# Recurrent block: three output blocks taken from raw tokens and scaled in PSUM, the tokens normalised in place meanwhile

## The chip, the cores and the metric

The kernel runs on one core of one Trainium2 chip. The metric is the device time of one execution in microseconds, as the median of the runs. The engines are named as in the profile: PE (matmuls; PEld its weight loads), DVE (VectorE), ACT (ScalarE), POOL (GpSimd) and SP (which issues the DMAs; SPq is its queue).

## The reference

A two-layer trunk on 1024 tokens of width 1024, in float32. Layer one is a recurrent block and an MLP, layer two banded attention and an MLP; each part is normalised first and added to the stream. Only the recurrent block's beginning is touched:

```
def rmsnorm(x, g):
    y = xf * lax.rsqrt(jnp.mean(xf * xf, axis=-1, keepdims=True) + EPS)
    return (y * g.astype(jnp.float32)).astype(x.dtype)

def recurrent_block(x, w_in, conv_w, conv_b, w_gate, b_gate, lam, w_out):
    u = x @ w_in
    gate, rec = u[..., :D_RNN], u[..., D_RNN:]
    rec = causal_depthwise_conv(rec, conv_w, conv_b)
    h = rg_lru(rec, w_gate, b_gate, lam)
    return (jax.nn.gelu(gate) * h) @ w_out

h = h + recurrent_block(rmsnorm(h, a_norm[l]), a_w_in[l], ...)
```

The norm's factor, one number per token, is the same for all 1024 features of that token, so it can be multiplied into x before the product with w_in or into the product after it.

## The kernel before, in words

Everything lies transposed: features on the 128 partitions, tokens along the free axis. x is eight feature blocks (k = 0 to 7) of 1024 tokens, and each is handled as two halves (h = 0, 1) of 512 tokens. w_in has sixteen output blocks of 128 columns: eight for the gate, eight for the recurrence. The weights of one output block come in two halves of 128x512 (y = 0 for k = 0 to 3, y = 1 for k = 4 to 7).

Float32 products are made of three float32r matmuls: each operand is split into a high part (ACT, a copy that rounds, L487 for weights, L589 for tokens) and a low part (DVE, the difference, L489 and L592), and `mm` (L334 to L336) adds high by high, low by high and high by low in PSUM. One `mm` of 512 tokens is three matmuls; one output block over all k and both halves is 48.

The stage is written as many small chains (Python generators) that a planner, `Plan`, runs in the order of planned times. It gives every operation a cost and a due time (`a_`, `d_`, `p_` are the planned costs on ACT, DVE and POOL), flags and counting semaphores hold chains back, and the order in which the planner reaches the operations is the order in each engine's queue on the chip. The engines work their queues in order; the planner knows nothing of engines that hold one another up. Because the order is fixed at build time, an instruction that is late on the chip also holds what stands behind it in its queue.

The chains around the change:

- `loads` (L494) issues the DMAs on SP: first the first half of x (eight blocks), then the weights of the first two output blocks with the small vectors between them, then the second half of x with the third block's weights, then all other weights. Raw weights have three buffers (`NRAW_A`), and each is free again when DVE has made the low part.
- `square` (L538): ACT squares each token block, DVE adds the squares up (L551).
- `rstd` (L555): PE sums the squares over the partitions (L559), ACT takes Ln, Exp and a Square (L563, L565, L569), and DVE makes one Newton step (L571, L574), which gives R[h], the negated factor. It sets `normal[h]`.
- `halve` (L580): once the norm of half h is there, DVE multiplies the token block by R[h] in place (L585), ACT makes the high part times the negated gain (L589), DVE the low part (L592).
- `constants` (L414): some 25 instructions on 128x8 tiles, mostly on DVE (L416), among them a polynomial for softplus; the tanh and exponential of the recurrence use them (sp4, sp8).
- `tensor` (L712) is PE's order: the first three output blocks (recurrence 0 and 1, gate 0) go together through half 0 and then half 1, each in a PSUM tile of its own (`recs`); then a loop in which one recurrence block (n + 1) goes ahead, followed by the gate matmuls of recurrence n - 1 (L746) and a gate block. The fourth output block, the first in the loop, takes the same parts of the tokens as the first three. `block` (L691) goes through one output block by weight halves.
- `conv` (L596) takes a finished recurrence block out of PSUM with one ACT pass (L602) and three DVE passes (L609), and makes parts of the result (L618, L620); `gate` (L668) takes the gelu; `lru` (L624) makes the recurrence, on ACT, DVE and POOL.
- Before the first real work, PE runs 24 warm-up matmuls (`WARM`, L1293) on constants.

There are four PSUM tiles of 1024 columns in this stage, seven SBUF buffers for wide intermediate results (`bs`) and ten for split weights (`wss`).

Of the kernel before, what the change touches and what calls it, by code (L numbers as in the profile page):

```python
# [18 lines left out]
NF = 8  # L19
# [11 lines left out]
NW_A = 10  # L31
BANKS = {"pj": 2, "tp": 3, "po": 1, "sc": 2}
PIN = 0
WARM = 24
START = 48
SLACK = 14
ROWS = 2
# [120 lines left out]
def tile_yoco_rglru_chunk_attention(  # L158
# [42 lines left out]
    def gf(s="g"):  # L201
        return gp.tile([P, H2], F32, tag="g", name=nm(s))
# [34 lines left out]
    def hs(h):  # L237
        return slice(h * H2, (h + 1) * H2)
# [175 lines left out]
    def constants():  # L414
        def small(f, *args, **kw):
            f(*args, **kw)  # L416
            return plan.use("dve", 0.2)

        yield plan.t
        yield small(dve.tensor_scalar, gneg, vec[:, V_AN, :], -1.0, None, ALU.mult)  # L420
        dve.tensor_scalar(e0, lam, -1.0, None, ALU.mult)
# [3 lines left out]
        yield small(dve.tensor_scalar, e2, e1, 2.0, None, ALU.add)  # L425
        yield small(dve.reciprocal, e2, e2)
        yield small(dve.tensor_tensor, e1, e1, e2, ALU.mult)
        yield small(dve.tensor_tensor, e2, e1, e1, ALU.mult)
        yield small(dve.tensor_scalar, sps, e2, 1.0 / 19, 1.0 / 17, ALU.mult, ALU.add)
# [5 lines left out]
        yield small(dve.tensor_scalar, sp4, sps, 4.0, None, ALU.mult)  # L435
        yield small(dve.tensor_scalar, sp8, sps, -8.0, None, ALU.mult)
        yield arrived[NF - 1, 1]
        yield small(dve.tensor_scalar, gq, hn[:, 0:1], 0.125, None, ALU.mult)
        yield small(dve.tensor_scalar, gk, hn[:, 1:2], -1.0, None, ALU.mult)
# [17 lines left out]
    normal, gated = flags(2), flags(NF + 1)  # L457
    conved, posted, hidden, out_y = flags(NF), flags(NF + 2), flags(NF), flags(NF)
    xin, xsq, W, recs, C, HID, GW = {}, {}, {}, {}, {}, {}, {}
    Y = [[None, None] for _ in range(NF)]  # L460
# [31 lines left out]
        weighed[i, y].set(last)  # L492

    def loads():  # L494
        for k in range(NF):
            xin[k, 0] = gf("x")
            dma(xin[k, 0], xT[k, :, hs(0)])
            arrived[k, 0].set(plan.load(H2))
        for i in range(2):
            for y in range(2):  # L500
                yield raws
                load_half(i, y)
            if i == 0:
                dma(vec, vecs)
                plan.start(constants(), plan.load(NVEC * NF * 2) + 1.0)
        for k in range(NF):
            xin[k, 1] = gf("x")
            dma(xin[k, 1], xT[k, :, hs(1)])
            arrived[k, 1].set(plan.load(H2))
            if k == 3:  # L510
                dma(hn, hnorm)
                for y in range(2):
                    yield raws
                    load_half(2, y)
# [22 lines left out]

    def square(k, h):  # L538
        yield arrived[k, h]
        if (k, h) == (0, 1):  # L540
            yield normal[0,]
        elif h:
            yield squared[k - 1, h]
        yield bs
        q = bf("acc")[:, hs(0)]
        if k == 0:
            xsq[0, h] = q
        act.activation(q, xin[k, h], AF.Square)
        yield plan.use("act", a_(H2))
        if k:  # L550
            dve.tensor_tensor(xsq[0, h], xsq[0, h], q, ALU.add)  # L551
            bs.release(plan.use("dve", d_(H2)))
        squared[k, h].set(plan.busy["dve"] + LAT if k else plan.t)

    def rstd(h):  # L555
        yield squared[NF - 1, h]
# [20 lines left out]
        bs.release(last)  # L577
        normal[h,].set(last)

    def halve(k, h):  # L580
        yield normal[h,]
        if k:
            yield halved[k - 1, h]
        x = xin[k, h]
        dve.tensor_tensor(x, x, R[h], ALU.mult)  # L585
        yield plan.use("dve", d_(H2))
        hi, lo = gr("h"), gr("l")
        g = gneg[:, k : k + 1]
        act.activation(hi, x, AF.Copy, scale=g)  # L589
        X[k][h] = (hi, lo)  # L590
        yield plan.use("act", a_(H2))
        dve.scalar_tensor_tensor(lo, x, g, hi.bitcast(F32), ALU.mult, ALU.subtract)  # L592
        halved[k, h].set(plan.use("dve", d_(H2)))


    def conv(n, ps):  # L596
# [91 lines left out]
        xs.release(last)  # L688
        out_y[n,].set(last)

    def block(ps, i, Z, ks, start, stop):  # L691

        for y in range(2):
            mine = [k for k in ks if k // 4 == y]
            if not mine:
                continue
            yield weighed[i, y]
            for h in range(2):
                for k in mine:
                    if Z is Y:  # L700
                        yield out_y[k,]
                    w = W[i, y]
                    mm(
                        ps[:, hs(h)], (w[0][:, k % 4, :], w[1][:, k % 4, :]), Z[k][h],
                        start and k == ks[0], stop and k == ks[-1],
                    )
                    yield plan.pe(3 * H2) - LAT
            if i not in IN_G and mine[-1] % 4 == 3:
                wss.release(plan.now)
                wss.release(plan.now)  # L710

    def tensor():  # L712
# [575 lines left out]
    with tc.manual_schedule(engines=set(ENG)):  # L1288

        idle = bank2()[:, hs(0)]  # L1290
        wide = onesr.unsqueeze(1).broadcast_to([P, 4, P])
        for x in range(WARM):
            pe.matmul(idle, lhsT=onesr, rhs=wide, start=x == 0, stop=x == WARM - 1)  # L1293
        plan.start(loads())
        plan.start(gate_weights())
        for h in range(2):
            for k in range(NF):
                plan.start(square(k, h))
            plan.start(rstd(h))
            for k in range(NF):  # L1300
                plan.start(halve(k, h))
        plan.start(tensor())
        plan.start(o1.loads())
        plan.run()
# [497 lines left out]
```

## Time and profile before

| what | value |
|---|---|
| median of 3 runs (lowest, highest) | 2134.49 us (2132.64, 2136.97) |
| span of the profiled execution | 2134.0 us, 0.5 us under the median |
| PE, DVE, ACT, POOL busy in the span | 2091.0, 1546.1, 1106.3, 578.6 us |
| first 63 us: PE, DVE, ACT, POOL busy | 48.34, 43.56, 33.90, 2.81 us |
| first real matmul starts | 19.72 us |
| first gate matmul starts | 73.85 us |

A time is given from the start of the span. In a row of the timeline stand the start, the time that it took, the engine, the line of the kernel, the operation and its output and input tiles; in brackets the idle time of the engine before it and what ended that. In the table by stages, each engine's busy time stands with its count of instructions, then the granted PE clock (1.00 is full speed), the DMA share and the bandwidth. In the groups of instructions, the count is followed by the total, the mean in ns, and the idle time ahead. A row can carry the line of a helper: all three matmuls of a product have L334 to L336, whichever block they belong to.

### The profile page before, as it was taken

To read this page: it belongs to the slowest core of one execution; us is meant where nothing else is said; L and a number is where in the kernel's file an instruction comes from. 1 tells how busy PE (TensorE), PEld (TensorE's weight loads), DVE (VectorE), ACT (ScalarE), POOL (GpSimd) and SP (SyncE) were. 2 spreads that over 40 slices of the span, in tenths; PEclk is the share of its full clock that TensorE was granted. 3 is DMA by queue.
4 is the path that set the end of the run, shared out by engine and by line. 5 is a ranking of instruction groups with operands and counts; after the bars stand their busy time and mean duration, and the time that the engine had idled before them with its cause. 6 is when DMAs were issued, how large, how long until landed. Compare 5 with 4: busy or idle time off the path is not lost.

```text
span 2134.0 us, 29347 instructions
## 1 busy us (share of the span) xinstructions
PE 2091.0 (98%) x9768; PEld 1733.2 (81%) x9768; DVE 1546.1 (72%) x2602; ACT 1106.3 (52%) x1965; POOL 578.6 (27%) x511
## 2 busy tenths in 40 slices
PE   7999999999999999999999999989999999999999
PEld 5788787888888888887888888878778888888887
DVE  7777768777777776647777877767787777777743
ACT  5777635434434545546666666764544343444631
POOL 0123202333310000127666666650133332000000
PEclk9999999999999999999999999999999999999999
DMA  4111324544469784534323332343364445987732
GB/s 139 35 50 50 128 94 168 183 149 154 157 230 317 234 264 131 163 109 111 87 73 97 91 96 79 88 151 127 103 215 144 158 154 174 332 263 245 241 107 94
DMA packets 174296, 319.21 MB, mean 150 GB/s; under 512 B 20544, under 2 KB 22592, under 8 KB 174144
## 3 DMA queue, kind: packets, MB, share of 16 engines
q1 hardware_dynamic: 174144, 317.33, 45.8%
q8 instruction: 77, 1.26, 0.3%
q14 instruction: 75, 0.61, 0.1%
HBM read 219.73 MB, written 78.64 MB: 140 GB/s over the span
## 4 chain that ended last, share of the span: by engine, by line
PE 87%; DVE 6%; ACT 3%; issue 2%; DMA 1%; POOL 1%; SPq 0%; DVEq 0%; ACTq 0%; POOLq 0%
PE pj L334 12%; PE pj L336 11%; PE pj L335 11%; PE tp L334 6%; PE tp L336 6%; PE tp L335 6%; PE sc L336 4%; PE sc L335 4%; PE sc L334 4%; PE p L335 3%; PE p L334 3%; PE p L336 3%; PE tp L1583 2%; PE po L1611 2%; PE po L1610 1%
## 5 line engine op out<-in xcount | busy, mean ns | idle before, releaser
L334 PE MATMUL pj<-h,wh 128*128 128x512 f32 x1198 | 482.6, 403 | 4.5 <-DVE s L1118 3.7
L335 PE MATMUL pj<-l,wh 128*128 128x512 f32 x1198 | 468.7, 391 | 0.7 <-POOL l L1636 0.7
L336 PE MATMUL pj<-h,wl 128*128 128x512 f32 x1198 | 468.5, 391 | 0.2
L1037 ACT ACTIVATE wh<-raw 128x512 fp32r<-128x512 f32 x349 | 219.0, 629 | 318.2 <-PE po L335 80.6
L1038 DVE TENSOR_TENSOR wl<-raw,wh 128x512 fp32r<-128x512 f32 x349 | 270.2, 777 | 102.6 <-ACT wh L1037 99.1
L334 PEld LDWEIGHTS pj<-h,wh 128*128 128x128 f32 x1198 | 226.4, 189 | 48.3 <-DVE s L1118 4.9
L336 PEld LDWEIGHTS pj<-h,wl 128*128 128x128 f32 x1198 | 225.3, 188 | 49.0 <-DVE wl L1038 1.0
L335 PEld LDWEIGHTS pj<-l,wh 128*128 128x128 f32 x1198 | 226.6, 189 | 38.9 <-POOL l L1636 1.4
L334 PE MATMUL tp<-h,wh 128*128 128x512 f32 x569 | 221.8, 390 | 0.0
L335 PE MATMUL tp<-l,wh 128*128 128x512 f32 x569 | 221.6, 390 | 0.0
L336 PE MATMUL tp<-h,wl 128*128 128x512 f32 x569 | 221.6, 389 | 0.0
L348 DVE TENSOR_TENSOR l<-raw,h 128x512 fp32r<-128x512 f32 x224 | 154.1, 696 | 28.4 <-ACT h L347 26.9
L336 PE MATMUL sc<-h,wl 128*128 128x512 f32 x425 | 166.4, 392 | 0.0
L347 ACT ACTIVATE h<-raw 128x512 fp32r<-128x512 f32 x224 | 137.4, 620 | 56.1 <-DMA raw<-hid 32.7
L335 PE MATMUL sc<-l,wh 128*128 128x512 f32 x425 | 166.4, 391 | 0.0
L334 PE MATMUL sc<-h,wh 128*128 128x512 f32 x425 | 166.1, 391 | 0.0
L334 PE MATMUL p<-h,wh 128*128 128x512 f32 x384 | 151.7, 395 | 12.5 <-ACT h L589 8.1
L1119 ACT ACTIVATE s<-s 128x512 f32<-128x512 f32 x125 | 78.4, 629 | 164.4 <-DVE s L1118 164.4
L1046 POOL TENSOR_TENSOR raw<-raw,raw 128x512 f32<-128x512 f32 x30 | 49.7, 1657 | 405.3 <-DVE wl L1038 398.2
L335 PE MATMUL p<-l,wh 128*128 128x512 f32 x384 | 151.3, 394 | 3.0 <-DVE l L592 2.7
L336 PE MATMUL p<-h,wl 128*128 128x512 f32 x384 | 150.3, 391 | 0.0
L294 POOL TENSOR_TENSOR raw<-raw,vec 128x512 f32<-128x512 f32 x48 | 54.8, 1142 | 262.9 <-DVE l L348 259.6
(276 smaller groups left out, 4206.3 us busy)
## 6 DMA issues: line engine op xcount, KB each, us to landing
raw<-hid SPq DMA_DIRECT2D x224, 256.0 KB, 3.6
hid<-s SPq DMA_DIRECT2D x221, 256.0 KB, 2.1
raw<-in_w_down SPq DMA_DIRECT2D x192, 256.0 KB, 3.5
raw<-in_w_up SPq DMA_DIRECT2D x128, 256.0 KB, 2.6
s<-in_w_down SPq DMA_DIRECT2D x64, 256.0 KB, 4.3
raw<-in_w_in SPq DMA_DIRECT2D x32, 256.0 KB, 2.7
raw<-in_w_kv SPq DMA_DIRECT2D x32, 256.0 KB, 3.3
od<-ev SPq DMA_DIRECT2D x48, 128.0 KB, 2.2
```

The lines of the kernel that those rows point to most:

```text
L294: pool.tensor_tensor(raw, raw, gains, ALU.mult)
L334: pe.matmul(ps, lhsT=wh, rhs=xh, start=start, stop=False, skip_group_check=more)
L335: pe.matmul(ps, lhsT=wh, rhs=xl, start=False, stop=False, skip_group_check=more)
L336: pe.matmul(ps, lhsT=wl, rhs=xh, start=False, stop=stop, skip_group_check=more)
L347: act.activation(h, src, AF.Copy)
L348: dve.tensor_tensor(l, src, h.bitcast(F32), ALU.subtract)
L1037: act.activation(wh, raw, AF.Copy)
L1038: dve.tensor_tensor(wl, raw, wh.bitcast(F32), ALU.subtract)
L1046: pool.tensor_tensor(raw[A11], raw[A11], raw[A21], ALU.add)
L1119: act.activation(out, out, AF.Square)
L1583: pe.transpose(pt[:, g * P : (g + 1) * P], sc[:, (kb - kb0) * P : (kb - kb0 + 1) * P], ident)
L1611: pe.matmul(out, lhsT=st, rhs=pl[:, off : off + wid], start=False, stop=y == final)
```

## The change

The norm no longer stands ahead of the first three output blocks.

- `part` (new): as soon as a token block and the gains are there, ACT and DVE make the high and low parts of the raw tokens times the negated gain. The first three output blocks use these.
- `scaled_later` (new): when the three blocks are done, DVE multiplies each half of each of the three PSUM tiles by R[h], six instructions, and then the convolution or the gelu goes on as before.
- `halve`: the product with R[h] in place now waits also for `spent`, PE's use of the raw parts. It runs on POOL, but for k = 3 and 7 of the first half on DVE. ACT and DVE then make the parts again, in the same tiles. The fourth output block and all later ones use these.
- `square`: of the first half ACT still squares, and POOL adds; of the second half POOL squares and DVE adds.
- `constants`: most of the small instructions go from DVE to POOL.
- `loads`: the vectors go first, then tokens of the first half in turn with the weights of the first three blocks, then all of the second half.
- `block`: the fourth output block goes through half 0 and then half 1 over all k, and each product waits for its own parts.
- `WARM`: 12 rather than 24.

The diff, cut to its core:

```
-WARM = 24
+WARM = 12
...
+        def aside(f, *args, **kw):
+            f(*args, **kw)
+            return plan.use("pool", 0.25)
...
-        yield small(dve.tensor_scalar, gneg, vec[:, V_AN, :], -1.0, None, ALU.mult)
+        gained[0,].set(small(dve.tensor_scalar, gneg, vec[:, V_AN, :], -1.0, None, ALU.mult))
+        yield arrived[NF - 1, 0]
...
         for m in (15, 13, 11, 9, 7, 5, 3, 1):
-            yield small(dve.tensor_tensor, sps, sps, e2, ALU.mult)
-            yield small(dve.tensor_scalar, sps, sps, 1.0 / m, None, ALU.add)
+            yield aside(pool.tensor_tensor, sps, sps, e2, ALU.mult)
+            yield aside(pool.tensor_scalar, sps, sps, 1.0, 1.0 / m, ALU.mult, ALU.add)
...
     def loads():
...
+        dma(vec, vecs)
+        plan.start(constants(), plan.load(NVEC * NF * 2))
+        token_block(0, 0)
+        for y, ks in ((0, (1, 2, 3)), (1, (4, 5, 6))):
+            for i, k in zip(range(3), ks):
                 yield raws
                 load_half(i, y)
+                token_block(k, 0)
+        token_block(NF - 1, 0)
         for k in range(NF):
+            token_block(k, 1)
+        dma(hn, hnorm)
...
     def square(k, h):
...
-        act.activation(q, xin[k, h], AF.Square)
-        yield plan.use("act", a_(H2))
+        if h:
+            pool.tensor_tensor(q, xin[k, h], xin[k, h], ALU.mult)
+            yield plan.use("pool", p_(H2))
+        else:
+            act.activation(q, xin[k, h], AF.Square)
+            yield plan.use("act", a_(H2))
         if k:
-            dve.tensor_tensor(xsq[0, h], xsq[0, h], q, ALU.add)
+            (dve if h else pool).tensor_tensor(xsq[0, h], xsq[0, h], q, ALU.add)
...
+    def part(k, h):
+        yield gained[0,]
+        yield arrived[k, h]
         x = xin[k, h]
         hi, lo = gr("h"), gr("l")
         g = gneg[:, k : k + 1]
         act.activation(hi, x, AF.Copy, scale=g)
         X[k][h] = (hi, lo)
         yield plan.use("act", a_(H2))
         dve.scalar_tensor_tensor(lo, x, g, hi.bitcast(F32), ALU.mult, ALU.subtract)
+        parted[k, h].set(plan.use("dve", d_(H2)))
+
+    def halve(k, h):
+        yield normal[h,]
+        yield spent[k, h]
+        x = xin[k, h]
+        if not h and k % 4 == 3:
+            dve.tensor_tensor(x, x, R[h], ALU.mult)
+            yield plan.use("dve", d_(H2))
+        else:
+            pool.tensor_tensor(x, x, R[h], ALU.mult)
+            yield plan.use("pool", p_(H2))
+        hi, lo = X[k][h]
+        g = gneg[:, k : k + 1]
+        act.activation(hi, x, AF.Copy, scale=g)
+        yield plan.use("act", a_(H2))
+        dve.scalar_tensor_tensor(lo, x, g, hi.bitcast(F32), ALU.mult, ALU.subtract)
         halved[k, h].set(plan.use("dve", d_(H2)))
+
+    def scaled_later(ps, then):
+        for h in range(2):
+            yield normal[h,]
+            dve.tensor_tensor(ps[:, hs(h)], ps[:, hs(h)], R[h], ALU.mult)
+            yield plan.use("dve", d_(H2))
+        yield from then
...
     def tensor():
...
                 for x in range(3):
                     yield weighed[x, k // 4]
-                    yield halved[k, h]
+                    yield parted[k, h]
...
+                spent[k, h].set(plan.now)
...
-        plan.start(conv(0, recs[0]))
-        plan.start(gate(0, recs[2]))
-        plan.start(conv(1, recs[1]))
+        plan.start(scaled_later(recs[0], conv(0, recs[0])))
+        plan.start(scaled_later(recs[2], gate(0, recs[2])))
+        plan.start(scaled_later(recs[1], conv(1, recs[1])))
...
-                yield from block(ps, widx[NF + n + 1], X, allk, True, True)
+                yield from block(ps, widx[NF + n + 1], X, allk, True, True, n == 1)
```

More of the change, by code (lines that the diff above doesn't have):

```diff
@@ L417, in small @@
             return plan.use("dve", 0.2)
+        def aside(f, *args, **kw):
+            f(*args, **kw)
+            return plan.use("pool", 0.25)
         yield plan.t
[L420 to L421 removed]
+        gained[0,].set(small(dve.tensor_scalar, gneg, vec[:, V_AN, :], -1.0, None, ALU.mult))
+        yield arrived[NF - 1, 0]
+        yield aside(pool.tensor_scalar, e0, lam, -1.0, 1.0, ALU.mult, ALU.mult)
         yield small(dve.tensor_tensor, e1, e0, lam, ALU.max)
@@ L424, in constants @@
         yield plan.use("act", 0.25)
-        yield small(dve.tensor_scalar, e2, e1, 2.0, None, ALU.add)
+        yield aside(pool.tensor_scalar, e2, e1, 1.0, 2.0, ALU.mult, ALU.add)
         yield small(dve.reciprocal, e2, e2)
-        yield small(dve.tensor_tensor, e1, e1, e2, ALU.mult)
-        yield small(dve.tensor_tensor, e2, e1, e1, ALU.mult)
-        yield small(dve.tensor_scalar, sps, e2, 1.0 / 19, 1.0 / 17, ALU.mult, ALU.add)
+        yield aside(pool.tensor_tensor, e1, e1, e2, ALU.mult)
+        yield aside(pool.tensor_tensor, e2, e1, e1, ALU.mult)
+        yield aside(pool.tensor_scalar, sps, e2, 1.0 / 19, 1.0 / 17, ALU.mult, ALU.add)
         for m in (15, 13, 11, 9, 7, 5, 3, 1):
-            yield small(dve.tensor_tensor, sps, sps, e2, ALU.mult)
-            yield small(dve.tensor_scalar, sps, sps, 1.0 / m, None, ALU.add)
+            yield aside(pool.tensor_tensor, sps, sps, e2, ALU.mult)
+            yield aside(pool.tensor_scalar, sps, sps, 1.0, 1.0 / m, ALU.mult, ALU.add)
         yield small(dve.scalar_tensor_tensor, sps, sps, 2.0, e1, ALU.mult, ALU.mult)
         yield small(dve.scalar_tensor_tensor, sps, e0, 0.0, sps, ALU.max, ALU.add)
-        yield small(dve.tensor_scalar, sp4, sps, 4.0, None, ALU.mult)
-        yield small(dve.tensor_scalar, sp8, sps, -8.0, None, ALU.mult)
+        yield aside(pool.tensor_scalar, sp4, sps, 4.0, 1.0, ALU.mult, ALU.mult)
+        yield aside(pool.tensor_scalar, sp8, sps, -8.0, 1.0, ALU.mult, ALU.mult)
         yield arrived[NF - 1, 1]
-        yield small(dve.tensor_scalar, gq, hn[:, 0:1], 0.125, None, ALU.mult)
-        yield small(dve.tensor_scalar, gk, hn[:, 1:2], -1.0, None, ALU.mult)
+        yield aside(pool.tensor_scalar, gq, hn[:, 0:1], 0.125, 1.0, ALU.mult, ALU.mult)
+        yield aside(pool.tensor_scalar, gk, hn[:, 1:2], -1.0, 1.0, ALU.mult, ALU.mult)
     def a_(n):
@@ L456, in tile_yoco_rglru_chunk_attention @@
     weighed = flags(3 * NF, 2)
-    normal, gated = flags(2), flags(NF + 1)
+    normal, gained = flags(2), flags(1)
+    parted, spent = flags(NF, 2), flags(NF, 2)
     conved, posted, hidden, out_y = flags(NF), flags(NF + 2), flags(NF), flags(NF)
@@ L494, in loads, with token_block @@
     def loads():
[L495 to L500, printed above, removed]
+        def token_block(k, h):
+            xin[k, h] = gf("x")
+            dma(xin[k, h], xT[k, :, hs(h)])
+            arrived[k, h].set(plan.load(H2))
+        dma(vec, vecs)
[3 more added lines that the diff above has]
+            for i, k in zip(range(3), ks):
                 yield raws
                 load_half(i, y)
-            if i == 0:
-                dma(vec, vecs)
-                plan.start(constants(), plan.load(NVEC * NF * 2) + 1.0)
+                token_block(k, 0)
+        token_block(NF - 1, 0)
         for k in range(NF):
[L507 to L514, printed above, removed]
+            token_block(k, 1)
+        dma(hn, hnorm)
         for i in range(3, 3 * NF):
@@ L539, in square @@
         yield arrived[k, h]
[L540 to L543, printed above, removed]
         yield bs
@@ L547, in square @@
             xsq[0, h] = q
-        act.activation(q, xin[k, h], AF.Square)
-        yield plan.use("act", a_(H2))
+        if h:
[4 more added lines that the diff above has]
+            yield plan.use("act", a_(H2))
         if k:
-            dve.tensor_tensor(xsq[0, h], xsq[0, h], q, ALU.add)
-            bs.release(plan.use("dve", d_(H2)))
-        squared[k, h].set(plan.busy["dve"] + LAT if k else plan.t)
+            (dve if h else pool).tensor_tensor(xsq[0, h], xsq[0, h], q, ALU.add)
+            last = plan.use("dve", d_(H2)) if h else plan.use("pool", p_(H2))
+            bs.release(last)
+        squared[k, h].set(last if k else plan.t)
     def rstd(h):
@@ L578, in rstd @@
         normal[h,].set(last)
[L580 to L583, printed above, removed]
+    def part(k, h):
+        yield gained[0,]
+        yield arrived[k, h]
         x = xin[k, h]
-        dve.tensor_tensor(x, x, R[h], ALU.mult)
-        yield plan.use("dve", d_(H2))
         hi, lo = gr("h"), gr("l")
@@ L689, in gate, with block @@
         out_y[n,].set(last)
[L691 to L696, printed above, removed]
-            yield weighed[i, y]
[L698 to L708, printed above, removed]
+    def block(ps, i, Z, ks, start, stop, halves=False):
+        ys = [[k for k in ks if k // 4 == y] for y in range(2)]
+        if halves:
+            order = [(h, k) for h in range(2) for k in ks]
+        else:
+            order = [(h, k) for mine in ys for h in range(2) for k in mine]
+        for h, k in order:
+            y = k // 4
+            yield weighed[i, y]
+            if Z is Y:
+                yield out_y[k,]
+            else:
+                yield halved[k, h]
+            w = W[i, y]
+            mm(
+                ps[:, hs(h)], (w[0][:, k % 4, :], w[1][:, k % 4, :]), Z[k][h],
+                start and k == ks[0], stop and k == ks[-1],
+            )
+            yield plan.pe(3 * H2) - LAT
+            if i not in IN_G and h == 1 and k == ys[y][-1] and k % 4 == 3:
                 wss.release(plan.now)
@@ L1300, in tile_yoco_rglru_chunk_attention @@
             for k in range(NF):
+                plan.start(part(k, h))
+            for k in range(NF):
                 plan.start(halve(k, h))
```

## The prediction

> **What bounds the kernel now.** I read the page first, then the busy time by stages, then the waits, then the single instructions of the first 100 us.
>
> ```profile
> span 2134.0 us, 29347 instructions
> PE 2091.0 (98%) x9768; PEld 1733.2 (81%) x9768; DVE 1546.1 (72%) x2602; ACT 1106.3 (52%) x1965; POOL 578.6 (27%) x511
> core 0: us, PE busy (x) PEld busy (x) DVE busy (x) ACT busy (x) POOL busy (x), PEclk, DMA share, GB/s
> 0.00:5.00 5.00, 4.02 (x10) 3.15 (x11) 0.00 (x0) 2.41 (x3) 1.24 (x11) 1.00 0.51 166
> 10.00:15.00 5.00, 1.12 (x2) 0.30 (x2) 4.17 (x9) 4.02 (x9) 0.00 (x0) 0.87 0.46 148
> 15.00:20.00 5.00, 0.28 (x1) 0.28 (x1) 4.20 (x12) 3.04 (x5) 0.00 (x0) 0.50 0.78 219
> 20.00:25.00 5.00, 4.18 (x9) 2.49 (x9) 3.11 (x7) 2.33 (x4) 0.00 (x0) 0.60 1.04 369
> 45.00:63.00 18.00, 18.00 (x81) 14.86 (x81) 11.03 (x17) 7.82 (x11) 0.00 (x0) 1.00 0.08 28
> 90.30:93.60 3.30, 0.07 (x2) 0.07 (x1) 3.30 (x4) 3.06 (x4) 2.20 (x3) 1.00 0.29 89
> 93.60:200.00 106.40, 106.40 (x470) 88.12 (x470) 81.39 (x70) 79.52 (x88) 25.92 (x13) 1.00 0.16 51
> ```
>
> PE is the bound, at 98% of the span. All that the change can touch lies before about 94 us: from 93.6 to 200 PE is busy 106.40 of 106.40 us. So whatever moves PE's arrival there moves the end by as much. The last row also gives the pace of a matmul: 106.40 / 470 = 0.226 us.
>
> Two rows date PE's work in the recurrent block, and two its waits:
>
> ```profile
> 19.72 0.79 PE L334 MATMUL p<-h,wh 128*128 128x512 f32 x1 [6.30 <-ACT h L589]
> 73.85 0.39 PE L334 MATMUL p<-ch,gw 128*128 128x512 f32 x1
> PE p L334 <- ACT h L589: 8.1, 4, 6.3
> PE p L334 <- DVE c L609: 3.2, 1, 3.2
> ```
>
> The first real matmul starts at 19.72, after the norm of the first half. The first gate matmul starts at 73.85. Ahead of it stands the fourth output block (48 matmuls, 10.9 us, so it began at 63.0), and ahead of that the first three (144 matmuls, 32.6 us, from 19.72 to 63.0: 10.7 us of it waits and the slow clock of the rows from 15 to 25). 73.85 is my yardstick: the time at which the changed kernel reaches the same gate matmul.
>
> **The change part by part.** *PE's start.* The first three blocks no longer wait for the norm. They wait for the gains, one half block of tokens and a split weight.
>
> ```profile
> 3.88 1.23 ACT L548 ACTIVATE acc<-x 128x512 f32<-128x512 f32 x2 [1.87 <-DMA x<-in_xT]
> 6.91 3.93 ACT L548 ACTIVATE acc<-x 128x512 f32<-128x512 f32 x6 [1.80 <-DMA x<-in_xT]
> vec<-in_vecs SPq DMA_DIRECT2D x1, 52.0 KB, 4.7
> L589 ACT ACTIVATE h<-x,gneg 128x512 fp32r<-128x512 f32 x16 | 11.4, 720 | 17.6 <-DVE x L585 17.6
> ```
>
> The vectors now go first: issued at 0.7, landing 4.7 later, 5.4; gains and high part (0.72) after it: about 6.3; the first tokens are there before that (ACT squares them from 3.88). Twelve warm-up matmuls at the pace of the first ten (4.02 / 10 = 0.4 us in the row from 0 to 5, from about 1.0 on) end at about 5.8, so halving the warm-up costs nothing. With 32.6 us of work PE could be through with three blocks at about 40 to 45, some 18 to 20 us earlier. That is the gain on offer. But the fourth block takes normalised tokens, as all later ones do, and needs the last low part of the second half's eighth block. So the yardstick is set by how fast DVE, ACT and POOL make two complete sets of parts in place of one.
>
> *What DVE and POOL have to do.* Before, DVE did the products with the norm, the additions of squares, the low parts and the weights' low parts. Now POOL does 7 additions, 8 squares and 14 of 16 products, and DVE 16 more low parts. The question is whether the two run side by side. The trace has stretches in which both are loaded:
>
> ```profile
> 359.44 1.61 POOL L1049 TENSOR_TENSOR raw<-raw,raw 128x512 f32<-128x512 f32 x1 [3.10 <-DVE wl L1038]
> 359.82 1.78 DVE L1038 TENSOR_TENSOR wl<-raw,wh 128x512 fp32r<-128x512 f32 x1
> 361.13 1.62 POOL L1051 TENSOR_TENSOR raw<-raw,raw 128x512 f32<-128x512 f32 x1
> 361.52 1.78 DVE L1168 TENSOR_TENSOR raw<-raw,raw 128x512 f32<-128x512 f32 x1
> 371.25 1.59 POOL L1047 TENSOR_TENSOR raw<-raw,raw 128x512 f32<-128x512 f32 x1
> 371.63 0.68 DVE L1154 TENSOR_TENSOR s<-pj,s 128x512 f32<-128x512 f32 x1
> 41.76 1.29 DVE L585 TENSOR_TENSOR x<-x,rneg 128x512 f32<-128x512 f32 x2
> 43.24 1.42 DVE L592 SCALAR_TENSOR_TENSOR l<-x,gneg,h 128x512 fp32r<-128x512 f32 x2 [0.19 <-ACT h L589]
> L1058 POOL TENSOR_TENSOR raw<-raw,raw 128x512 f32<-128x512 f32 x1 | 1.3, 1302 | 4.4 <-DMA raw<-in_w_up 4.4
> L1389 POOL TENSOR_TENSOR s<-q x32: 1034/1042/1487, 951.2 to 1376.3; 128x512 f32<-128x512 f32 x32
> ```
>
> Around 360 the two take turns: each DVE instruction with both inputs in SBUF grows from 0.69 to 1.78 us and ends 0.55 after POOL's, and each POOL instruction from 1.30 to 1.61. One of each costs 361.13 - 359.44 = 1.69 us. At 371.63 a DVE instruction whose one input is PSUM runs through a POOL instruction at its usual 0.68. So DVE instructions with two SBUF inputs and POOL's exclude one another. Alone, DVE's follow at 1.29 - 0.69 = 0.60 us and the low parts at 1.42 - 0.75 = 0.67, which leaves 1.69 - 0.60 = 1.09 for POOL's. A square (one tensor read twice) takes 1.04 rather than 1.30; less the same 0.2 of overhead, 0.84.
>
> The Trainium skill states the same ("SBUF — State Buffer", section "Who interferes with whom"): a VectorE instruction with two SBUF inputs and a GpSimd instruction that reads SBUF block each other, whole instructions at a time. By it the edit cannot spread this work over two engines, and the trace agrees (1.69 us a pair); engines running side by side would give the first rival's time.
>
> The sum, up to the last low part of the second half: DVE 32 low parts by 0.67 = 21.4, and 7 additions, 8 weight halves, 2 products and 2 last steps of the norm, 19 by 0.60 = 11.4: 32.8. POOL 21 by 1.09 = 22.9, 8 squares by 0.84 = 6.7, two gate weights of 256 columns by half of 1.09 = 1.1, eight small constants at 0.1 = 0.8 (bounds below): 31.5. Together 64.3 us of turns. They begin at 6.3 and end at 70.6 if neither ever waits. They will wait: the square root chain leaves a hole before the second half,
>
> ```profile
> 36.59 1.02 PE L559 MATMUL p<-acc,onesr 128*128 128x512 f32 x2
> 40.43 0.69 DVE L574 SCALAR_TENSOR_TENSOR rneg<-x,rneg 128x512 f32<-128x512 f32 x1
> ```
>
> 41.1 - 36.6 = 4.5 us each time. In the first, low parts of the second half fill it; in the second, only some four to six low parts do (3 to 4 us, DVE's alone), so 1 to 2 us stay. On SP the first half's tokens are now mixed with six weight halves of 256 KB (0.7 us each at the 369 GB/s of the row from 20 to 25), and weights wait for three raw buffers that DVE frees, the tokens behind them too; ACT squared the eighth block by 10.8, now I put it at 15 to 18, another 1 to 2 us of hole. Sum 72.6 to 74.6, and the last three matmuls 0.7: the yardstick comes at 73.3 to 75.3. I take 74.8, in the upper half, since DVE's queue also holds the norms' two steps from PSUM (bounds 71.3 without holes, 80.3 with both chains fully open), against 73.85: **+1.0**. PE's 18 us are given back waiting.
>
> *Scaling in PSUM.* Six DVE instructions with one input in PSUM:
>
> ```profile
> L1383 DVE SCALAR_TENSOR_TENSOR q<-pj,rneg 128x512 f32<-128x512 f32 x32 | 22.0, 688 | 14.2 <-PE pj L336 13.8
> L609 DVE SCALAR_TENSOR_TENSOR c<-p,vec,c 128x1022 f32<-128x1022 f32 x8 | 10.2, 1277 | 0.1
> L620 DVE TENSOR_TENSOR cl<-c,ch 128x1024 fp32r<-128x1024 f32 x8 | 9.8, 1220 | 1.9 <-ACT ch L618 1.2 <-PE p L336 0.7
> ```
>
> 6 by 0.6 = 3.6 us, beside POOL's turns. They and the first convolution's three passes (1.28 each) stand in DVE's queue among the low parts of the second half. I count them as covered by POOL's eight products (8 by 1.3 = 10.4 us). The gate matmuls also need the convolution's low part (1.22), which comes last: wait 0 to 3, I take **+1.0**.
>
> *Waits added.* A product waits for the norm and for PE's use of the old parts. Behind it in POOL's queue stand the constants, moved there from DVE, some 18 of them after the last product. Their price is in no row; the nearest:
>
> ```profile
> L1787 POOL MEMSET const-float32-0.0<- 128x1 f32 x1 | 0.1, 103 | 0.2 <-issue 0.2
> L1575 POOL TENSOR_SCALAR sc<-sc,t 128x128 f32<-128x128 f32 x16 | 7.0, 435 | 21.6 <-DVE t L1573 21.6
> 77.78 1.14 ACT L636 ACTIVATE tanh<-sig,sp 128x1024 f32<-128x1024 f32 x1
> ```
>
> 0.1 to 0.435; eight columns are nearer to one than to 128, so 0.2: 3.6 us (1.8 to 7.8). The first user is the tanh, 77.78 - 73.85 = 3.9 after the yardstick, and the last product ends about 2 before it: hidden, 0 to +2. The norm's matmul waits in PE's queue for POOL's and DVE's additions, with the rest of the three blocks behind it; PE has the slack.
>
> *Clock.* While PE waits for parts it may fall to the 0.5 of the row from 15 to 20; in the next row it is still 0.60. After the yardstick that would cost 0 to 2 us; I take **+0.5**. The 3.2 us wait at 90.3 for a convolution pass stays (bounds -3.2 and 0).
>
> Sum: 2134.0 + 1.0 + 1.0 + 0.5 = 2136.5 for the profiled execution, which lies 0.5 under the runs' median of 2134.5: **2137.0**. Bounds of this case, not all at one end together: 2131 to 2142.
>
> **The rivals.** *The engines overlap after all.* If short in-place instructions did not exclude one another, POOL's 29 instructions would run in 21 by 1.30 and 8 by 1.04, 35.6 us, DVE beside them; the second norm would be ready near 39, the last product near 50, and PE, through with three blocks at 44, would go straight into the fourth: the yardstick at 44 + 10.9 = 55, -19, hence 2115. For it speaks PE's real slack, against it the four rows at 360. Chance 0.14.
>
> *DVE's queue order decides: slower.* DVE takes its queue in order. If the six scalings and four convolution passes (3.6 + 4 by 1.2 = 8.4 us) come before the last low parts while POOL already stands idle, they are not covered but added: 2137.0 + 8.4 = 2145.4. It decides from the point where over 2 us of them remain when POOL's last product is done. For it speaks that the additions of POOL's slower turns push the second norm's DVE steps behind the first half's low parts; against it that POOL has 10.4 us of products in the same stretch. Chance 0.26.
>
> The forecast's case has 0.60.
>
> **How the numbers follow.** A measurement of this kernel can tell about 0.2%, 4.3 us, from no change (2130.2 to 2138.8). Of the forecast's 0.60, 0.05 falls under that (the 3.2 us wait gone as well) and 0.12 above. Faster: 0.14 + 0.05 = 0.19. Slower: 0.12 + 0.24 of the second rival = 0.36. Same: 0.45. The range, 2126 to 2146, leaves out nearly all of the first rival and the far end of the second, 0.2 together.
>
> **What would show it.** The first real matmul should start at 6 to 8 us rather than 19.72, and the three blocks be done by 45 to 60. Then PE should wait for low parts and the first gate matmul start near 75 to 76. Low parts that lie beside a POOL instruction should take 1.4 to 1.8 us, not 0.75, and POOL's products 1.6. POOL and DVE should take turns nearly without a gap from 8 to 70. From 94 on, all should be as before, shifted. A gate matmul at 55 to 60, with low parts at 0.75, would make me wrong the fast way; one at 80 or later, with PE or POOL idle behind DVE's scalings and convolutions, the slow way.

## The result, and the profile after

The changed kernel takes 2147.40 us (median of 4 runs, 2145.25 to 2147.95) against 2134.68 for the kernel before (4 runs, 2132.64 to 2136.97): a ratio of 1.0054, with a 95% interval of 1.0039 to 1.0068. It is slower, by more than twice the 0.2% that can be told from no change, and just past the upper end of the forecast's range. The second rival had 2145.4. The profiled execution took 2147.08, with a span of 2145.3 against 2134.0, so 11.3 us are to be explained.

The page of the changed kernel opens with the span and the engines' busy time. Below it, in a second fence, are rows of busy time by stage, with the columns of those of before:

```profile
span 2145.3 us, 29384 instructions
PE 2095.4 (98%) x9756; PEld 1734.2 (81%) x9756; DVE 1563.7 (73%) x2578; ACT 1110.0 (52%) x1973; POOL 633.3 (30%) x565
```

```profile
10.00:15.00 5.00, 3.74 (x17) 2.86 (x16) 5.00 (x4) 4.20 (x8) 4.39 (x4) 1.00 0.70 215
...
45.00:63.00 18.00, 15.13 (x62) 12.02 (x60) 17.97 (x19) 11.32 (x19) 15.82 (x13) 0.93 0.06 18
63.00:78.00 15.00, 10.49 (x23) 6.76 (x24) 15.00 (x16) 7.61 (x10) 10.26 (x19) 0.67 0.17 58
...
95.00:100.00 5.00, 0.89 (x4) 0.38 (x3) 5.00 (x5) 4.20 (x4) 4.48 (x3) 0.87 0.07 24
100.00:105.00 5.00, 4.11 (x10) 3.31 (x11) 4.97 (x3) 1.06 (x1) 1.76 (x1) 0.50 0.34 107
105.00:215.00 110.00, 110.00 (x486) 91.03 (x485) 78.29 (x73) 83.67 (x93) 26.00 (x13) 1.00 0.14 46
```

PE does run from the start now: 17 matmuls between 10 and 15, where there were two. DVE is busy for 17.97 of the 18 us from 45 to 63 and for all of the 15 after. The matmuls suffer there (62 where there were 81, then a granted clock of 0.67). Two more bad stretches follow, at 95 and at 100, and from 105 PE is full.

The timeline dates this. Each line has start, duration, engine and line, operation, and in brackets the idle time before it and what ended that. On PE:

```profile
7.77 0.50 PE L334 MATMUL p<-h,wh 128*128 128x512 f32 x1 [0.52 <-ACT wh L493]
78.08 0.46 PE L334 MATMUL p<-ch,gw 128*128 128x512 f32 x1
100.89 0.77 PE L334 MATMUL p<-h,wh 128*128 128x512 f32 x1 [5.00 <-DVE c L634]
```

PE's waits between 5 and 210, the largest groups (us in total, times, longest):

```profile
PE p L335 <- DVE l L610: 7.3, 2, 4.8
PE p L334 <- DVE c L634: 5.0, 1, 5.0
...
PE p L335 <- DVE cl L645: 0.9, 1, 0.9
```

The first real matmul comes at 7.77 rather than 19.72, and yet the first gate matmul, the yardstick, comes at 78.08 rather than 73.85. The loss adds up along PE: +4.23 us at the yardstick; +0.92 for the first convolution's low part (the third wait); +1.8 because the wait of 3.2 us at 90.3 is now one of 5.0 at 95.9; and about 2 for the matmuls behind it, which run at half the clock (from 100 to 105 ten of them take 4.11 us, at full pace 10 by 0.226 = 2.3). A gate matmul that stood at 216.09 then stands at 225.58: +9.49, of which these four give 9.0 and a lower clock around the yardstick the rest. The last 1.8 us of the 11.3 arise later. PE has two new waits of 1.3 us there, the first at 331.61; what causes them is open.

Why the yardstick is late is read from DVE and POOL. First the groups of DVE and POOL instructions up to 77.5 (count, then busy us and mean ns of one):

```profile
L593 DVE SCALAR_TENSOR_TENSOR l<-x,gneg,h 128x512 fp32r<-128x512 f32 x16 | 16.9, 1084 | 1.9 <-ACT h L590 1.8
...
L610 DVE SCALAR_TENSOR_TENSOR l<-x,gneg,h 128x512 fp32r<-128x512 f32 x16 | 17.7, 1155 | 0.0
L495 DVE TENSOR_TENSOR wl<-raw,wh 128x512 fp32r<-128x512 f32 x12 | 13.4, 1119 | 0.8 <-ACT wh L493 0.8
L616 DVE TENSOR_TENSOR p<-p,rneg 128x512 f32<-128x512 f32 x6 | 3.9, 684 | 0.0
L604 POOL TENSOR_TENSOR x<-x,rneg 128x512 f32<-128x512 f32 x14 | 23.2, 1685 | 3.4 <-DVE rneg L578 3.4
```

Low parts (L593 raw, L610 normalised) and weight halves (L495) take 1.08 to 1.16 us in the mean rather than 0.69 to 0.75, POOL's products 1.69 (a mean of 14 from 1.29 to 1.75). Only the six scalings, with one input in PSUM, stay at 0.68. The turns are there as forecast. Now how POOL ends, and what DVE does afterwards:

```profile
66.74 1.67 POOL L604 TENSOR_TENSOR x<-x,rneg 128x512 f32<-128x512 f32 x1
```

```profile
63.77 5.19 DVE L610 SCALAR_TENSOR_TENSOR l<-x,gneg,h 128x512 fp32r<-128x512 f32 x4
68.89 1.27 DVE L634 SCALAR_TENSOR_TENSOR c<-p,vec,c 128x1021 f32<-128x1021 f32 x1
...
71.36 2.46 DVE L634 SCALAR_TENSOR_TENSOR c<-p,vec,c 128x1022 f32<-128x1022 f32 x2
73.74 1.40 DVE L610 SCALAR_TENSOR_TENSOR l<-x,gneg,h 128x512 fp32r<-128x512 f32 x2
75.06 1.27 DVE L634 SCALAR_TENSOR_TENSOR c<-p,vec,c 128x1023 f32<-128x1023 f32 x1
76.26 0.74 DVE L610 SCALAR_TENSOR_TENSOR l<-x,gneg,h 128x512 fp32r<-128x512 f32 x1
```

POOL's last product ends at 68.41. The last low part, on which the yardstick hangs, ends at 77.0. In the 8.1 us from 68.9 DVE does four low parts (4 by 0.67), one weight half (0.6) and four convolution passes (4 by 1.2 = 4.8) that stand between them: the three of the first convolution and one of the second.

### The profile page after: what moved, and what is told of

The parts are those of the page before. It is cut to its first block, busy times and chain, and to the rows that moved or that the text cites. A ratio compares the mean times of both kernels' runs of the same rounds, so it can differ in the third digit from the quotient of the medians.

```text
span 2145.3 us, 29384 instructions
## 1 busy us (share of the span) xinstructions
PE 2095.4 (98%) x9756; PEld 1734.2 (81%) x9756; DVE 1563.7 (73%) x2578; ACT 1110.0 (52%) x1973; POOL 633.3 (30%) x565
## 4 chain that ended last, share of the span: by engine, by line
PE 84%; DVE 8%; ACT 3%; issue 2%; DMA 2%; POOL 1%; SPq 0%; DVEq 0%; POOLq 0%; ACTq 0%
PE pj L334 11%; PE pj L335 11%; PE pj L336 11%; PE tp L336 6%; PE tp L334 6%; PE tp L335 6%; PE sc L336 4%; PE sc L335 4%; PE sc L334 4%; PE p L335 3%; PE p L334 3%; PE p L336 3%; PE tp L1614 2%; PE po L1642 2%; PE po L1641 1%
```

## The experiments

Three theories were held against each other. *Theory 1*, the turns: DVE and POOL exclude one another, so the work handed to POOL costs time instead of saving it. *Theory 2*, the queue: the order in which DVE's and ACT's queues are filled puts work ahead of what PE waits for. *Theory 3*: the new order of transfers and the shorter warm-up. The changed kernel is the base unless something else is said. Each ratio is against the kernel before as it ran beside that experiment; its median lay between 2134.68 and 2136.77, so a difference between the medians of two experiments is good to some 2 us. "Low part" is the end of the last normalised low part (77.0 in the changed kernel), "yardstick" the first gate matmul (78.08; 73.85 before).

### All products on DVE

```
-        if not h and k % 4 == 3:
+        if True:
```

> The changed kernel with all 16 products with the norm on DVE instead of 14 of them on POOL; the squares and additions stay on POOL. Theory 1 (turns: a POOL product holds DVE's low parts up for 1.09 us, on DVE it costs 0.60): 14 x 0.49 = 6.9 us less up to the last low part, which ended at 77.0 and would end near 70; the first gate matmul, 78.1, comes near 71 to 73 and the time is 5 to 7 us under the changed kernel's 2147. Theory 2 (DVE's queue: what counts is how much stands in it, and POOL's products are free for it): 14 x 0.60 = 8.4 us more in that queue, the first gate matmul at 84 to 87, the time 6 to 9 us above 2147. Theory 3 (the new order of transfers or the shorter warm-up costs the time): no difference.

Measured: 2147.99 us, ratio 1.0059 (1.0044 to 1.0074). The low part came at 71.1, 5.9 us earlier although DVE had 14 instructions more. That part of theory 1 held; its time did not. The time is what theory 3 had said (no difference), but theory 3 does not move the low part. From the timelines of PE and DVE:

```profile
78.27 0.79 PE L334 MATMUL p<-ch,gw 128*128 128x512 f32 x1 [5.46 <-ACT ch L643]
```

```profile
71.04 7.22 DVE L634 SCALAR_TENSOR_TENSOR c<-p,vec,c 128x1021 f32<-128x1021 f32 x6
```

The yardstick now waited 5.46 us for the first convolution. Its passes stood behind all low parts, in turn with those of the second one, and the 5.9 us were gone. So both theories have a hand in it: with the products' turns lifted, the queue decides.

### POOL out of it: squares and additions too

The same edit, and the second half squared on ACT, all additions on DVE:

```
-        if h:
+        if False:
...
-            (dve if h else pool).tensor_tensor(xsq[0, h], xsq[0, h], q, ALU.add)
-            last = plan.use("dve", d_(H2)) if h else plan.use("pool", p_(H2))
+            dve.tensor_tensor(xsq[0, h], xsq[0, h], q, ALU.add)
+            last = plan.use("dve", d_(H2))
```

> As the run with all products on DVE, and besides the second half's squares on ACT and all additions on DVE: POOL keeps only the small constants and the gate weights. Theory 1 (turns): 8 squares by 0.84 leave the turns and 7 additions get cheaper by 0.49, together 10 us less than there; but the first norm then also stands behind ACT, which has 32 high parts and 16 squares to do, so not all of it shows: first gate matmul at 62 to 70, the time 8 to 16 us under the changed kernel's 2147, at or below the kernel before. Theory 2 (length of DVE's queue): 7 more additions, 4 us slower than the run with all products on DVE. Theory 3: no difference.

Measured: 2137.51, ratio 1.0010 (1.0000 to 1.0019), 10 us under the changed kernel. Low part 61.1, yardstick 68.36. The groups of DVE up to 62, same instructions, same counts as above:

```profile
L593 DVE SCALAR_TENSOR_TENSOR l<-x,gneg,h 128x512 fp32r<-128x512 f32 x16 | 11.8, 744 | 2.6 <-ACT h L590 2.5
L610 DVE SCALAR_TENSOR_TENSOR l<-x,gneg,h 128x512 fp32r<-128x512 f32 x16 | 11.1, 747 | 0.5 <-ACT h L608 0.5
...
L495 DVE TENSOR_TENSOR wl<-raw,wh 128x512 fp32r<-128x512 f32 x12 | 8.1, 686 | 1.0 <-ACT wh L493 1.0
```

The 44 instructions of these rows take DVE 31.0 us instead of 48.0, and though it now has all products and additions as well, it is through 15.9 us earlier. The yardstick, after a wait of 4.18 for the first convolution, leads the kernel before by 5.5 us. Most of that lead goes in the granted clock behind this wait, 0.56 to 0.59 from 68 to 76, and in 0.57 from 92 to 96, behind the wait for a convolution pass, which is still there with 2.9 us: the gate matmul of 216.09 comes at 215.70.

### All sixteen blocks from raw parts

In the block of the first three, all blocks use the raw parts, each one is scaled in PSUM, and `halve` is never started.

```
-                yield halved[k, h]
+                yield parted[k, h]
...
-                plan.start(conv(n + 1, ps))
+                plan.start(scaled_later(ps, conv(n + 1, ps)))
...
-            for k in range(NF):
-                plan.start(halve(k, h))
```

> The changed kernel without the second set of parts: all 16 output blocks are made from the raw parts and each is scaled in PSUM (26 more scalings by 0.6 us on DVE, spread over 130 us), 16 products, 16 high and 16 low parts gone. All theories that put the loss on the second set of parts (turns as well as DVE's queue) expect the fourth block to follow the third without a wait: three blocks done near 52 (two waits for the norms' sums stay in PE's queue), first gate matmul at 60 to 66, 12 to 18 us earlier than 78.1. If the later blocks' scalings (1.2 us a block on DVE beside PE at 10.9 us a block) stay hidden, the time is 2126 to 2135; if they lie on the path of convolution and gate, up to 13 x 1.2 = 16 us are lost again and it is 2140 to 2150. Theory 3 (transfers, warm-up): 2147.

Measured: 2136.29, ratio 1.0003 (0.9993 to 1.0012), between the two times that had been named. Yardstick 64.72, some 7 us ahead of the kernel before until 195; then a wait of 5.16 for a convolution's low part and a granted clock of 0.50 behind it, from 201 to 206, took the lead away. POOL's squares and additions were still in this one.

### Gate and second convolution behind the last low part

DVE's queue gets the scalings and passes of these two only after the last normalised low part; the first convolution stays where it was.

```
+    def behind(then):
+        yield halved[NF - 1, 1]
+        yield from then
...
-        plan.start(scaled_later(recs[2], gate(0, recs[2])))
-        plan.start(scaled_later(recs[1], conv(1, recs[1])))
+        plan.start(behind(scaled_later(recs[2], gate(0, recs[2]))))
+        plan.start(behind(scaled_later(recs[1], conv(1, recs[1]))))
```

> The changed kernel with one change of order: the scalings of the second and third block and what follows them (gate 0 and convolution 1) go into the queues only behind the last normalised low part. Theory 2 (DVE's queue order): four scalings (2.4 us) and two to three convolution passes (2.5 to 3.8) no longer stand ahead of the last low parts, so the last low part ends 4 to 6 us earlier (71 to 73 for 77.0), the first gate matmul 3 to 5 us earlier, and the sigmoid no longer waits in ACT's queue behind convolution 1: time 3 to 7 us under 2147. Theory 1 (turns alone): these instructions read PSUM and take no turn, so nothing moves by more than 1 us.

Measured: 2141.20, ratio 1.0025 (1.0015 to 1.0036), 6 us under the changed kernel, by order alone. The expected time came, but not in the expected way. The low part came at 75.5, 1.5 earlier where 4 to 6 had been said, and the yardstick gained only 0.9 (77.21). One convolution pass and four scalings had left the space ahead of the last low part; 1.5 is about the pass (1.2) alone, as if the scalings had cost nothing there, but single executions differ by nearly as much. The larger gain came later: the wait of 5.0 at 95.9 was gone, with one of 1.86 in its place:

```profile
83.06 0.50 PE L334 MATMUL p<-h,wh 128*128 128x512 f32 x1 [1.86 <-ACT sig L660]
```

So some 6 us of the 12.7 between the two medians hang on the queue, as theory 2 has it.

### The turns by themselves: POOL reads, POOL writes

Two kernels made from the one *before*, with useless work on POOL from about 17 us on that nobody waits for: sixteen squares, which read SBUF, or one square and eighteen fills, which only write.

```
+    def turns():
+        yield normal[0,]
+        yield xs
+        spare = xf("spare")
+        for _ in range(16):
+            pool.tensor_tensor(spare[:, :H2], R[0], R[0], ALU.mult)
...
```

```
+        pool.tensor_tensor(spare[:, :H2], R[0], R[0], ALU.mult)
+        for _ in range(18):
+            pool.memset(spare, 0.0)
...
```

> The kernel before, with 16 useless squares of the first norm's factor on POOL (128x512, SBUF to a spare buffer), queued from the first norm on (about 17 us) and needed by nobody. Theory 1 (turns: POOL's reads and DVE's instructions with two SBUF inputs exclude one another): while they run, DVE's products, additions and low parts grow from 0.69 and 0.75 to 1.4 us and more, POOL's squares from 1.04 to about 1.4; 16 x 0.84 = 13.4 us are taken from DVE, which had 3.6 us free from 20 to 45, so the first gate matmul, 73.85 before, comes 5 to 11 us later. Theory 2 (only the length of DVE's own queue counts): no row of DVE changes and the gate matmul stays within 1 us.

> The kernel before, with one square and then 18 fills of 128x1024 on POOL in the same place: POOL is about as long busy, but reads nothing. Theory 1 as stated (reads against two-input instructions): DVE's rows stay at 0.69 and 0.75 and the first gate matmul within 1 us of 73.85. If any busy POOL holds DVE up, it comes later as with the squares. Theory 2: within 1 us.

Measured, one run each: 2148.36 and 2134.47, beside a median of 2135.76 for the kernel before. Yardsticks 84.12 (10.3 later) and 72.11 (1.7 earlier, where at most 1 had been expected). Most of the 1.7 was there before the fills: ACT's split of the weights, which waits for their transfer, began at 20.54 rather than 21.75, and SyncE had issued that transfer from 14.65 rather than 15.68. So the yardsticks of single executions differ by a microsecond or more. In the first, POOL's squares and single DVE instructions among them, then DVE's additions of 17 to 45:

```profile
16.99 23.03 POOL L585 TENSOR_TENSOR spare<-rneg 128x512 f32<-128x512 f32 x16 [15.09 <-DVE e L416]
```

```profile
26.07 1.52 DVE L594 TENSOR_TENSOR x<-x,rneg 128x512 f32<-128x512 f32 x1
27.52 1.52 DVE L551 TENSOR_TENSOR acc<-acc,acc 128x512 f32<-128x512 f32 x1
28.96 1.00 DVE L416 TENSOR_TENSOR sps<-sps,e 128x8 f32<-128x8 f32 x1
```

```profile
L551 DVE TENSOR_TENSOR acc<-acc,acc 128x512 f32<-128x512 f32 x6 | 7.5, 1244 | 0.0
```

In the second, POOL's fills over much of the same time, and DVE's additions in the same stretch:

```profile
18.54 18.17 POOL L586 MEMSET spare<- 128x1024 f32 x18
```

```profile
L551 DVE TENSOR_TENSOR acc<-acc,acc 128x512 f32<-128x512 f32 x7 | 4.8, 685 | 0.0
```

An addition takes 1244 ns beside POOL's squares and 685 beside its fills, as in the kernel before. So POOL being busy is not enough: an instruction that reads shuts out DVE instructions with two SBUF inputs, a fill does not. This shows the turns apart from the order of any queue: sixteen reading instructions that nobody needs put the yardstick off by 10.3 us, and the one run's time by 12.6. The rule that the prediction took from the Trainium skill ("SBUF — State Buffer", section "Who interferes with whom") says just this, that such an instruction contends with a GpSimd instruction that reads, not with one that only writes; these two traces agree with it.

### All raw, and POOL out of it

The two edits together: all sixteen blocks from raw parts, squares on ACT, additions on DVE.

> As the run with all blocks made from raw parts, and besides the second half's squares on ACT and all additions on DVE, as in the run with POOL free. Theory 1: the turns that the squares and additions took (10 us) are free as well; the first norm comes at 31 to 33, PE does not wait at its two sums, the three blocks are done at 42 to 46 and the first gate matmul comes at 55 to 60 for 64.7. Behind that the later blocks' scalings decide, as there: it lost its whole lead at the wait of 5.2 us near 200. If that wait is bound to DVE's load, it takes the lead again and the time is 2134 to 2138; if not, 2126 to 2131. Theory 2: DVE has 7 additions more in its queue, 0 to 4 us slower than there.

Measured: 2124.19, ratio 0.9949 (0.9935 to 0.9964): faster than both kernels, 12 us under the all-raw kernel with POOL in it, 23 under the changed one. Yardstick 54.48. PE's busy time from the first real matmul to there (columns as above):

```profile
8.00:54.50 46.50, 45.64 (x194) 36.18 (x194) 35.18 (x56) 32.49 (x53) 10.85 (x26) 1.00 0.44 140
```

PE is full (45.64 of 46.50) at the whole clock. This has the change's transfers and its twelve warm-up matmuls, so theory 3 has little left: they allow a start without a single wait of a microsecond. They were not tried alone. Two waits still cost, both for a convolution's low part: one of 2.88 at 57.75, and the longer one at 191:

```profile
191.15 0.80 PE L335 MATMUL p<-cl,gw 128*128 128x512 f32 x1 [5.17 <-DVE cl L645]
```

### A fourth block from raw parts, POOL out of it

From the kernel with POOL out of it: the fourth block raw as well, the products made in place while it runs.

```
-        yield spent[k, h]
+        yield parted[k, h]
         x = xin[k, h]
...
+        yield spent[k, h]
         hi, lo = X[k][h]
...
-                yield from block(ps, widx[NF + n + 1], X, allk, True, True, n == 1)
-                plan.start(conv(n + 1, ps))
+                yield from block(ps, widx[NF + n + 1], X, allk, True, True, n <= 2, n == 1)
+                plan.start(scaled_later(ps, conv(n + 1, ps)) if n == 1 else conv(n + 1, ps))
```

> As the run with POOL free, but the fourth block also takes the raw parts and is scaled in PSUM, and the products with the norm are made ahead, in place, as soon as the norm is there (the raw parts do not need the tokens any more); only the high and low parts wait for PE. So PE has 43.5 us of work that waits for no norm, and behind it the new parts must come at 0.68 us each for the fifth block. Theory 1 with theory 2 (turns, and what stands in DVE's queue): first gate matmul at 57 to 63; the fifth block waits 0 to 6 us for low parts behind DVE's scalings and convolutions; the lead over the kernel before at the second gate matmuls (87.45) is 5 to 12 us, and the time 2123 to 2132, below both kernels. If the first norm or the transfers (theory 3) held PE up instead, the first gate matmul would stay at 68.

Measured: 2139.64, ratio 1.0016 (1.0006 to 1.0026), a miss. The yardstick's row:

```profile
70.46 0.79 PE L334 MATMUL p<-ch,gw 128*128 128x512 f32 x1 [14.30 <-ACT ch L644]
```

PE waited 14.30 us for the first convolution. With the products due earlier the planner put all sixteen low parts (49 to 62) into DVE's queue ahead of the two convolutions' passes (62.6 to 70.4). No theory had said so beforehand, but it is theory 2 again: removing a wait of PE let the queue's order make a longer one.

### The two kernels with POOL out of it, in another order

Gate 0 and convolution 1 behind the first convolution (`yield conved[0,]` in `behind`), first with all blocks raw, then with three.

> As the run with all blocks from raw parts and POOL free (2124 us), but gate 0 and convolution 1 go into the queues only when convolution 0 is done, so that convolution 0's three passes stand alone on DVE rather than in turn with convolution 1's. Theory of the queue's order: its low part, which ended at 57.7 and kept the first gate matmuls waiting 2.9 us, comes 3 us or more earlier; that wait goes, and the slow clock behind it (0.83 from 55 to 65): 3 to 5 us earlier at the second gate matmuls (72.8). The wait of 5.2 us near 191 has another cause and stays: 2119 to 2123. If the order of these instructions does not matter, 2124.

> As the run with the products, squares and additions off POOL but normalised tokens from the fourth block on (2137.5 us), with the same change of order: gate 0 and convolution 1 behind convolution 0. There the last normalised low part ended at 61.1 and the first gate matmul came at 68.4, having waited 4.2 us for convolution 0. Theory of the queue's order: that wait falls to 0 to 1 us, the first gate matmul comes at 63 to 65, and the time at 2131 to 2134, at or just below the kernel before. If what limits it is the turns alone, nothing moves: 2137.

Measured: 2126.28, ratio 0.9952 (0.9938 to 0.9967), and 2130.31, ratio 0.9966 (0.9954 to 0.9979). The first is a miss: no gain over 2124.19. An early wait of 2.9 became three of 4.3 us together, and the late one of 5.16 stayed. The second gained 7 us over the same kernel without the order (2137.51) and beats the kernel before. Its yardstick:

```profile
64.17 0.50 PE L334 MATMUL p<-ch,gw 128*128 128x512 f32 x1 [2.94 <-ACT ch L647]
```

The wait for the first convolution went from 4.18 to 2.94, where 0 to 1 had been expected, and the yardstick from 68.36 to 64.17.

## Why the prediction was wrong

*What held.* The first matmul came when forecast (7.77; 6 to 8), though by luck: the gains that were to set it were there at 2.9, and it waited for the split weight. As forecast were also the three blocks done by 54.5 (45 to 60), POOL's products (1.69; 1.6), low parts longer beside them (5.19 for four at 63.77, 1.3 each; 1.4 to 1.8), scalings untouched by POOL (0.68), a DVE that is full from 45 on, PE's start given back whole, and the wait for the convolution's low part (0.92; +1.0). The first rival, engines side by side, is out: the reading and the writing POOL tell it apart.

*What failed.* The step "I count them as covered by POOL's eight products". The scalings were: they ran between 56.9 and 63.8, beside products. The convolution passes were not. POOL's products ended at 68.41 and four of the passes, 4.8 us, came afterwards, ahead of the last low part. That is the second rival's mechanism, and its point of decision (over 2 us left when POOL's last product is done) was passed with 4.8. That its 2145.4 lies near the measured time is partly chance: it put all its 8.4 us ahead of the yardstick, which came 3.3 us behind my 74.8; the rest arose later. Four more weight halves than the eight of my sum (12 by the L495 row, 2.4 us more) stood in DVE's queue too. With both, 6.3 + 64.3 + 2.4 + 4.8 = 77.8, for a last low part at 77.0, so the sum's holes of 2 to 4 us are not needed: while DVE stood still for 2.19 us before 25, POOL was busy throughout. The kernel with all products on DVE adds a caution: with those passes *behind* the low parts PE waits for the convolution instead. The passes had no free place in DVE's queue, and "covered" would have needed a DVE with slack, which from 45 to 78 it never had. How the loss divides between the passes and the weight halves was not tried.

*What was mis-sized.* Of the 9.5 us at 225, the yardstick has 4.2 (forecast +1.0). The wait at 90.3, forecast to stay at 3.2, grew to 5.0: it hangs on a chain through DVE's and ACT's queues. The convolution pass that PE waits for stands in DVE's queue behind work on the recurrence, which needs the gate's sigmoid from ACT; it started at 99.47, where the kernel before had it at 92.15. And ACT's conversion for the second convolution, ahead of the gate's sigmoid in its queue, waited 3.20 us for DVE:

```profile
80.69 1.06 ACT L643 ACTIVATE ch<-c 128x1024 fp32r<-128x1024 f32 x1 [3.20 <-DVE sps L416]
```

The sigmoid behind it started at 83.06, where the kernel before had it at 75.41. The clock took about 2 rather than 0.5: behind the longer wait the granted clock was 0.50 for five us, where behind the one of 3.2 it had been 1.00. The step from span to median was mis-sized too: the prediction took the 0.5 of the kernel before, and in the changed one the median lies 2.1 above the span (2147.40 against 2145.3).

*How much belongs to which.* Taking POOL out gained 10 us with three raw blocks and 12 with sixteen. Leaving out the second set of parts gained 11 with POOL and 13 without. Moving two chains in the queue gained 6 with POOL (behind the last low part) and 7 without (behind the first convolution), but nothing with all blocks raw. The shares overlap, as the first experiment shows: lifting the products' turns alone gained nothing. Both together beat the kernel before by 6.5 us (2130.31 against 2136.77), and POOL out of it without the second set of parts by 11.6 (2124.19 against 2135.76).

*Open.* The 1.8 us after 225. The wait near 191 of the all-raw kernels: in the faster one a gate's scaling, which waited 2.35 us for PE, stands ahead of the convolution's third pass in DVE's queue; the pass ended at 174.07, ACT converted its result only at 183.74, behind other work, and DVE's low part came at 189.88, behind other work again. This is read from the trace and was not tried. The transfers and the warm-up were not tried alone.

## What to carry to other kernels

Before giving half of a full engine's work to an idle one, look for a stretch of the trace in which both already run, and price a pair of instructions there; here DVE's own 44 instructions grew from 31 to 48 us beside the helper, which is more than the 21 products and additions that it took over (14.4 us at 0.685). When a wait of PE is lifted, read the queue of the engine that feeds it instruction by instruction up to the one PE needs: what stands between decides, and a long instruction is only hidden if its engine has slack. Try the new idea without the helper first: raw tokens and scaling in PSUM, for all sixteen blocks, were worth 11 us here once POOL kept out of it; for three blocks 6.5, and only in another order.

## What the runs showed of the hardware

Small instructions pay for the turns out of all proportion. POOL's constants take 0.20 us beside DVE's convolution passes, which have an input in PSUM, and 0.5 to 0.67 beside its low parts and weight halves, as two rows of the changed kernel show (DVE did low parts at 66.14 and a pass at 69.81):

```profile
66.14 0.52 POOL L420 TENSOR_SCALAR sps<-sps 128x8 f32<-128x8 f32 x1
...
69.81 0.20 POOL L420 TENSOR_SCALAR sps<-sps 128x8 f32<-128x8 f32 x1
```

A DVE multiplication of eight columns took 1.00 us beside POOL's squares (at 28.96, above). And one kind of DVE instruction with a single SBUF input is held up by POOL's *writes*. The answers for the constants' line on DVE from 22 to 45, with shortest, median and longest ns, first in the kernel with the fills, then in the kernel before:

```profile
L416 DVE TENSOR_SCALAR sps<-sps x8: 181/670/787, 21.8 to 34.9; 128x8 f32<-128x8 f32 x8
L416 DVE TENSOR_TENSOR sps<-sps,e x7: 157/161/168, 23.7 to 34.7; 128x8 f32<-128x8 f32 x7
```

```profile
L416 DVE TENSOR_SCALAR sps<-sps x8: 159/164/731, 23.0 to 36.6; 128x8 f32<-128x8 f32 x8
```

Beside the fills the median of the `tensor_scalar` instructions is 670 ns instead of 164, while the two-input instructions between them, of the same size, stay at 161. The same section of the Trainium skill counts `tensor_scalar` among those that can use both ports of the shared pair and so contend with GpSimd; the trace fits that, though no run here shows which mode was used.
